# A prefill and decode layer with compensated one-pass products: last weight chunks of 21 input tiles and the narrow weights are split during the first feed-forward

## The chip, the cores and the metric

The kernel runs on one core of a Trainium2 chip. The metric is the device time of one launch in microseconds (us), as the median of several runs. PE is TensorE (matrix products), PEld its weight loads, DVE VectorE, ACT ScalarE, POOL GpSimd, SP SyncE, which here only issues transfers.

## The reference, cut to what matters

One layer of a hybrid decoder, in fp32, for 256 new tokens of one prompt and one new token each of 8 running sequences; together 264 columns:

```python
x = x + 0.5 * swiglu(rmsnorm(x, n1), f1g, f1u, f1d)      # 2048 -> 5504 -> 2048
h = rmsnorm(x, nm)
proj = h @ w_in                                          # 2048 -> 4864 columns
q, k, v = ...                                            # 16 query heads, 4 key/value heads of 64
o_att = attend(q, k, v, sinks)                           # window 128, sinks, relative bias
xm = proj + mu * (prev - proj)                           # token shift on the other 3328 columns
r, k, v, wl, al, gl = xm[...]
w = -softplus(-(w0 + tanh(wl) @ w2)) - 0.5               # decay:  64 -> 1024
a = sigmoid(a0 + al @ a2)                                # rate:   64 -> 1024
g = sigmoid(gl) @ g2                                     # gate:  128 -> 1024
S, y = wkv_scan(...)                                     # RWKV-7 state, 16 heads of 64
out = (groupnorm(y) + bonus) * g
x = x + concat(o_att, out) @ w_out
x = x + 0.5 * swiglu(rmsnorm(x, n2), f2g, f2u, f2d)
```

and a last rmsnorm; the new key/value windows, RWKV states and shift columns are outputs too.

## The kernel before, in words

All activations lie transposed: a tile holds 128 features by 264 columns, so the 2048 features are 16 tiles. Every large weight is used in 128 x 128 blocks. Each fp32 operand of a large product is written as a sum of two parts of the type fp32r, and three products of that type, which TensorE does as one instruction each, stand for the whole: hi x hi, hi x lo, lo x hi (`gemm`). Weights arrive in chunks of four blocks (128 x 512, 256 KB) over SyncE's queue into six buffers `raw`; ScalarE casts a chunk to `hi` (line 141) and VectorE subtracts to get `lo` (line 142 of the program, shown as its helper's line 68); there are four buffers of each (`chunk`). So a tile of a projection with 16 input tiles has 4 chunks and 48 products into one accumulator `acc`.

The program has three stages. The first feed-forward (`ffn`) goes over 43 hidden tiles in six parts: gate and up products for each hidden tile, then the down products of the part. Mixing (`mixing_body`) takes 38 tiles of `win`: tiles 0 and 1 are the inputs of decay, rate and gate, 2 to 25 the r, k, v of eight pairs of heads, 26 to 29 keys and values, 30 to 37 queries. The list `SEQ` sets their order: 0 to 19, then 26 to 33, then 20 to 25, then 34 to 37. After each chunk `tick` advances every running generator by one step, which strews the small work between the large products: `prep` for each pair (decay, rate, keys), `chain` for each batch of two pairs (the scan in blocks of 64), `attend` for each query tile, and so on. Then come the output projection and the second feed-forward. The engines' queues are filled in an order that a planner finds beforehand from estimated times; chunks have high priority in mixing.

Three products in mixing are done on plain fp32 operands, as one `mm` each, which TensorE's queue carries as two instructions: in `prep` the decay `tw` (65 rows: 64 of tanh(wl) and a row of ones that adds w0) and the rate `la` (128 rows, the first 64 meet zeros) by the pair's 128 x 256 weight `lw`; in `gnorm` the gate `sgl` by `g2s`. Their weights are loaded over SyncE's queue into a ring of `NLD` = 6 buffers `ld`, shared with the states, biases and cached keys. The block `o` holds squares for the norm at first and the eight query tiles later; block `e` is used late, by the output projection.

Of the kernel before, what the change touches and what calls it, by code (L numbers as in the profile page):

```python
# [7 lines left out]
F32 = mybir.dt.float32  # L8
F32R = mybir.dt.float32r
# [4 lines left out]
P = 128  # L14
# [15 lines left out]
NH, NQ, NT, NLD = 16, 8, 16, 6  # L30
# [21 lines left out]
VMU, VKK, VKA, VA0, VRK, VLW, VLB, VSK, VSD = 64, 90, 98, 106, 114, 122, 130, 138, 154  # L52
NVEC = 155
# [3 lines left out]
def body(tc, I, O):  # L57
# [51 lines left out]
    with ExitStack() as ctx:  # L109
# [35 lines left out]
        def gemm(ps, src, xs, step=None, rng=None, ahead=True, ready=None):  # L145
            n = len(xs)
            for k0 in range(0, n, CH):
# [3 lines left out]
                hi, lo = ready or chunk(src[:, k0 * P:k1 * P], k1 - k0, V, ahead)  # L151
# [160 lines left out]

        def first_ffn(n2):
# [8 lines left out]
            with tc.tile_pool(name="f1", bufs=1) as fp:  # L322
# [18 lines left out]
                ffn(n1, xr, I["gu1"], I["dn1"], nxt, load, more, None, first)  # L341
# [27 lines left out]
        def mixing_body(mx, n2, n3, XD, XR):  # L369
# [18 lines left out]
            tw = fix((65, T), "tw")  # L388
            G.memset(tw[64:65, :], 1.0)
# [8 lines left out]
            half = fix((P, 16), "half")  # L398
            ts(V, half, vec[:, VKA:VKA + 16], 0.5, ALU.mult)
# [30 lines left out]
            la, sgl = fix((P, T), "la"), fix((P, T), "sgl")  # L430
# [132 lines left out]
            def chain(bt):  # L563
# [121 lines left out]
                g2s = [load(I["g2"][bt.p0 + k], (P, P)) for k in range(n)]  # L685
# [16 lines left out]
            def gnorm(bt, pY, N, g2s):  # L702
# [207 lines left out]
            bat, att, bts, scores = [], [], [], []  # L910
            for kind, i in SEQ:
# [23 lines left out]
                else:  # L935
                    ps = win(LKV + 4 + i)
                    q = ob[i]
# [141 lines left out]

# [111 lines left out]
```

## Time and profile before

| | |
|---|---|
| median of 3 runs | 1935.28 us (1935.13 to 1935.48) |
| profiled execution | 1934.77 us, span 1932.9 us |
| granted TensorE clock | 0.998 |
| PE busy | 1919.4 us, 99% of the span |
| DVE, ACT busy | 1311.8 us (68%), 1023.7 us (53%) |
| DMA | 357 MB, 185 GB/s over the span |

The span runs from the first to the last instruction of the profiled execution; its own time has 1.9 us more around it. Busy time of an engine is the union of its instructions. A product's duration includes its way through the array, so successive products overlap and a mean duration is longer than the distance between their starts. In the chain of waits ("start us, length, what") each piece is followed back to what released it; a piece "PE acc L84 x61" is 61 products in a row that waited for nothing else. "<-" behind an idle time names what ended it.

### The profile page before, as it was taken

The page shows a single profiled execution, that of the slowest core. Times are in us where ns is not written, and L with a number is a line of the kernel's source. Part 1 is how long each engine was busy: PE and PEld are TensorE (multiplying, and loading weights), DVE is VectorE, ACT ScalarE, POOL GpSimd, SP SyncE. Part 2 cuts the span into 40 slices and gives each one's busy share as a digit, 9 for nine tenths or more (in the row PEclk, how much of TensorE's full clock was granted, in tenths as well). Part 3 has the DMA queues.
Part 4 walks back from the last instruction along what each step waited for, and adds up shares of the span by engine and source line. Part 5 has one row for each costly group of instructions (what it writes and reads, how often), then busy time and mean ns, then how long its engine had stood idle before and what let it go on. Part 6 is the DMA issues. An engine that isn't in the chain of part 4 may idle for free.

```text
span 1932.9 us, 45519 instructions
## 1 busy us (share of the span) xinstructions
PE 1919.4 (99%) x17171; PEld 1897.1 (98%) x17171; DVE 1311.8 (68%) x2606; ACT 1023.7 (53%) x2034; POOL 260.1 (13%) x376
## 2 busy tenths in 40 slices
PE   9999999999999999999999999999999999999998
PEld 9999999999999999999989999999999999999998
DVE  5865555655556568889988977866666666666665
ACT  5644444444444457675657555644444444444446
POOL 0401101011010113222102100300101001010012
PEclk9999999999999999999999999999999999999999
DMA  7666666666666668555646656666666666666664
GB/s 241 178 192 196 185 195 195 183 192 177 190 183 180 188 181 238 177 165 153 176 120 165 210 155 183 175 188 188 189 195 195 186 192 189 194 195 184 193 181 150
DMA packets 218464, 357.27 MB, mean 185 GB/s; under 512 B 33516, under 2 KB 71804, under 8 KB 218244
## 3 DMA queue, kind: packets, MB, share of 16 engines
q1 hardware_dynamic: 211936, 346.02, 60.8%
q10 hardware_dynamic: 6308, 8.35, 1.4%
q8 instruction: 134, 2.20, 0.4%
q14 instruction: 86, 0.70, 0.1%
HBM read 346.67 MB, written 9.69 MB: 184 GB/s over the span
## 4 chain that ended last, share of the span: by engine, by line
PE 96%; DVE 1%; ACT 1%; issue 1%; DMA 0%; POOLq 0%; POOL 0%; ACTq 0%; DVEq 0%
PE acc L84 89%; PE m L84 6%; DVE lo L68 0%; ACT t L78 0%; ACT hi L141 0%; DMA x<-in_x 0%; DVE t L801 0%; DVE st L68 0%; DVE Xt L68 0%; DMA ld<-in_bias 0%; ACT BT L533 0%; ACT L78 0%; POOLq L1187 0%; DVE PT L68 0%; PE m L528 0%
## 5 line engine op out<-in xcount | busy, mean ns | idle before, releaser
L68 DVE TENSOR_TENSOR lo<-raw,hi 128x512 fp32r<-128x512 f32 (+1 forms) x1288 | 874.0, 682 | 510.4 <-ACT hi L141 486.9
L141 ACT CAST hi<-raw 128x512 fp32r<-128x512 f32 (+1 forms) x1288 | 776.8, 606 | 820.2 <-PE acc L84 745.2
L84 PE MATMUL acc<-x,hi 128*128 128x264 f32 x4840 | 893.4, 286 | 0.8 <-ACT hi L141 0.8
L84 PEld LDWEIGHTS acc<-x,hi 128*128 128x128 f32 x4840 | 750.1, 189 | 4.3 <-ACT hi L141 1.0
L84 PE MATMUL acc<-x,lo 128*128 128x264 f32 x2420 | 691.3, 286 | 0.2 <-DVE lo L68 0.2
L84 PE MATMUL acc<-h,hi 128*128 128x264 f32 x2752 | 495.0, 284 | 0.0
L84 PEld LDWEIGHTS acc<-x,lo 128*128 128x128 f32 x2420 | 457.2, 189 | 2.7 <-issue 0.7
L84 PEld LDWEIGHTS acc<-h,hi 128*128 128x128 f32 x2752 | 424.4, 189 | 0.0
L84 PE MATMUL acc<-h,lo 128*128 128x264 f32 x1376 | 387.8, 284 | 0.0
L84 PEld LDWEIGHTS acc<-h,lo 128*128 128x128 f32 x1376 | 259.2, 189 | 0.0
L68 POOL TENSOR_TENSOR t<-t,t 128x264 f32<-128x264 f32 x74 | 79.8, 1078 | 1096.1 <-DVE t L68 949.8
L84 PE MATMUL acc<-y,hi 128*128 128x264 f32 x648 | 122.7, 284 | 0.0
L84 PE MATMUL acc<-o,hi 128*128 128x264 f32 x648 | 120.1, 284 | 0.0
L84 PE MATMUL acc<-kv,hi 128*128 128x264 f32 x582 | 109.8, 285 | 0.0
L84 PEld LDWEIGHTS acc<-y,hi 128*128 128x128 f32 x648 | 101.2, 189 | 0.1
L84 PEld LDWEIGHTS acc<-o,hi 128*128 128x128 f32 x648 | 100.1, 189 | 0.0
L71 DVE SCALAR_TENSOR_TENSOR x<-acc,x 128x264 f32<-128x264 f32 (+1 forms) x193 | 81.1, 425 | 24.3 <-PE acc L84 23.4
L84 PE MATMUL acc<-y,lo 128*128 128x264 f32 x324 | 92.0, 284 | 0.0
L84 PE MATMUL acc<-o,lo 128*128 128x264 f32 x324 | 92.0, 284 | 0.0
L84 PEld LDWEIGHTS acc<-kv,hi 128*128 128x128 f32 x582 | 89.9, 189 | 0.2
L68 DVE TENSOR_TENSOR t<-acc,t 128x264 f32<-128x264 f32 x156 | 67.4, 432 | 32.9 <-PE acc L84 32.9
L84 PE MATMUL acc<-kv,lo 128*128 128x264 f32 x291 | 82.9, 285 | 0.0
(307 smaller groups left out, 1592.5 us busy)
## 6 DMA issues: line engine op xcount, KB each, us to landing
raw<-in_gu SPq DMA_DIRECT2D x688, 256.0 KB, 3.4
raw<-in_dn SPq DMA_DIRECT2D x224, 256.0 KB, 2.9
raw<-in_win SPq DMA_DIRECT2D x152, 256.0 KB, 3.4
raw<-in_dn SPq DMA_DIRECT2D x160, 192.0 KB, 2.8
raw<-in_wout SPq DMA_DIRECT2D x64, 256.0 KB, 3.5
xsp<-x ACTq DMA_DIRECT2D x16, 132.0 KB, 3.4
x<-xsp SPq DMA_DIRECT2D x16, 132.0 KB, 4.2
ld<-in_sT SPq DMA_DIRECT2D x16, 128.0 KB, 3.6
```

The lines of the kernel that those rows point to most:

```text
L68: return e.tensor_tensor(out=out, in0=a, in1=b, op=op)
L71: return V.scalar_tensor_tensor(out=out, in0=a, scalar=s, in1=b, op0=op0, op1=op1)
L84: return TE.matmul(out, lhsT, rhs, start=start, stop=stop, **k)
L141: A.copy(hi[:, :w], raw[:, :w])
```

## The change

Four things change together.

1. `split_early` is a generator that the first feed-forward advances once per hidden tile from its second part on. Each step loads one 128 x 512 piece of weights (`er`), splits the piece loaded a step before (`eh`, `el`), and stores the parts that were split a step before that to DRAM. The first six pieces are the weights of decay, rate and gate (`low`); the other 21 are the last of the four chunks of tiles 3 to 19 and 26 to 29 of `win` (`AHEAD`, stored in `kept`). That is 27 loads, 27 splits and 54 stores.
2. In mixing, `win` fetches for each of these tiles both parts of its last chunk (128 x 1024, 512 KB, one transfer) one tile ahead into one of two halves of block `o`, and `gemm` uses them in place of a `chunk`. The query tiles take block `o` only when the first of them is computed.
3. The narrow products become one-pass. `lor` holds, for each of decay and rate, the high part of its 64 rows above their low part; the weight is stored twice, one below the other, so one product over 128 rows takes in both parts, and two (weight high, weight low) make the whole. The gate takes three products. w0 moves from a row of ones to the bias of the activation.
4. `NLD` becomes 8.

The queues, taken from the planned programs. First TensorE where the first pair's `prep` makes its decay and rate products (the names in a row are output <- moving operand, weight; `acc` is the win tile under way, the numbers are buffer names). Before:

```order
L84 MATMUL acc_10837<-x_106,lo_10840 128x264
L84 MATMUL m_10858<-tw,ld_10856 128x264
L84 MATMUL m_10860<-la,ld_10856 128x264
L84 MATMUL acc_10837<-x_107,hi_10872 128x264 x2
L84 MATMUL acc_10837<-x_107,lo_10873 128x264
```

and in the change:

```order
L85 MATMUL acc_11053<-x_108,lo_11057 128x264
L85 MATMUL m_11077<-e_10644,ld_11073 128x264
L85 MATMUL m_11077<-e_10644,ld_11075 128x264
L85 MATMUL m_11078<-e_10644,ld_11073 128x264
L85 MATMUL m_11078<-e_10644,ld_11075 128x264
L85 MATMUL acc_11053<-x_109,hi_11093 128x264 x2
L85 MATMUL acc_11053<-x_109,lo_11094 128x264
```

Two rows of plain fp32 (two instructions each) become four one-pass rows, `m_11077` the decay and `m_11078` the rate, at the same place in the tile. The gate of the first pair, in the change, with buffer numbers:

```order
L85 MATMUL acc2570_13685<-x32_108,hi2572_13687 128x264
L85 MATMUL m2520_13395<-gate0_10645,ld2466_13139 128x264
L85 MATMUL m2520_13395<-gate1_10646,ld2466_13139 128x264
L85 MATMUL m2520_13395<-gate0_10645,ld2467_13141 128x264
L85 MATMUL acc2570_13685<-x32_108,hi2572_13687 128x264
```

One row of plain fp32 has become three: high by high, low by high, high by low. Where the first kept chunk is used, TensorE's queue now reads it from block `o`:

```order
L85 MATMUL acc_10905<-x_110,hi_10944 128x264 x2
L85 MATMUL acc_10905<-x_110,lo_10945 128x264
L85 MATMUL acc_10905<-x_110,hi_10944 128x264 x2
L85 MATMUL acc_10905<-x_110,lo_10945 128x264
L85 MATMUL acc_10905<-x_111,o_10825 128x264 x12
L85 MATMUL acc_10979<-x_108,hi_10982 128x264 x2
```

The twelve products of that chunk follow those of the third chunk as before; only their source is another.

Second, SyncE's queue at the start of mixing (loads of `raw` are chunks, `ld` the ring). Before:

```order
L378 DMA ld_10856<-in_lw 128x256
L140 DMA raw_10637<-in_win 128x512
L378 DMA ld_11150<-in_lw 128x256
L140 DMA raw_10655<-in_win 128x512
L378 DMA ld_11414<-in_sT 128x256
L378 DMA ld_11416<-in_sT 128x256
L140 DMA raw_10680<-in_win 128x512
L378 DMA ld_11422<-in_sT 128x256
L378 DMA ld_11424<-in_sT 128x256
L140 DMA raw_10698<-in_win 128x512
```

In the change:

```order
L403 DMA ld_11073<-low 128x256
L141 DMA raw_10863<-in_win 128x512
L403 DMA ld_11075<-low 128x256
L141 DMA raw_10881<-in_win 128x512
L403 DMA ld_11356<-low 128x256
L403 DMA ld_11358<-low 128x256
L141 DMA raw_10907<-in_win 128x512
L443 DMA o_10825<-kept 128x1024 x2
L141 DMA raw_10925<-in_win 128x512
L403 DMA ld_11614<-in_sT 128x256
L403 DMA ld_11616<-in_sT 128x256
L403 DMA ld_11622<-in_sT 128x256
```

The narrow weights of the first two pairs are now two loads each, and the first two fetches of kept chunks stand between the chunks of the fourth tile, which has three chunks here. Later each fetch has a place of its own:

```order
L141 DMA raw_11165<-in_win 128x512
L141 DMA raw_11203<-in_win 128x512
L141 DMA raw_11221<-in_win 128x512
L141 DMA raw_11263<-in_win 128x512
L443 DMA o_10825<-kept 128x1024
L141 DMA raw_11281<-in_win 128x512
L141 DMA raw_11299<-in_win 128x512
L141 DMA raw_11338<-in_win 128x512
```

This fetch, the third, is for tile 5 and waits for the last product of tile 3, whose half it overwrites; ahead of it stand the chunk loads up to the first of tile 7. Counted through the whole queue, from the third fetch to the last there are 9 or 10 chunk loads ahead that belong to later tiles than the one waited for.

Third, SyncE's queue in the first feed-forward, around one step of `split_early`:

```order
L141 DMA raw_4215<-in_gu 128x512
L141 DMA raw_4233<-in_gu 128x512
L322 DMA kept<-eh_4101 128x512
L322 DMA kept<-el_4102 128x512
L141 DMA raw_4271<-in_gu 128x512
L332 DMA er_4269<-in_win 128x512
L141 DMA raw_4289<-in_gu 128x512
L141 DMA raw_4307<-in_gu 128x512
```

The two stores of one step stand together between the chunk loads of two hidden tiles, and the load of the next step follows one chunk load later; before the change there are only the chunk loads.

The diff, without the renumbering of a few columns and lines:

```diff
-NH, NQ, NT, NLD = 16, 8, 16, 6
+NH, NQ, NT, NLD = 16, 8, 16, 8
...
+AHEAD = [*range(3, 20), *range(26, 30)]
...
-        def gemm(ps, src, xs, step=None, rng=None, ahead=True, ready=None):
+        def gemm(ps, src, xs, step=None, rng=None, ahead=True, ready=None, kept=None):
...
-                hi, lo = ready or chunk(src[:, k0 * P:k1 * P], k1 - k0, V, ahead)
+                hi, lo = kept if kept and k1 == n else ready or chunk(src[:, k0 * P:k1 * P], k1 - k0, V, ahead)
...
+        def split_early(fp):
+            todo = [(I["win"][t][:, 12 * P:], [kept[i, :, e] for e in range(2)]) for i, t in enumerate(AHEAD)]
+            todo = [(I["low"][:, q * 512:(q + 1) * 512], [low[:, 2 * q:2 * q + 2, e] for e in range(2)]) for q in range(6)] + todo
+            raw, parts, keep = [], [], tc.keep_in_program_order
+            while todo or raw or parts:
+                if parts:
+                    to, both = parts.pop()
+                    for d, x in zip(to, both):
+                        keep(SP.dma_start(d, x.bitcast(F32) if len(d.shape) == 2 else x.bitcast(F32).rearrange("p (k c) -> p k c", k=2)))
+                if raw:
+                    to, x = raw.pop()
+                    hi, lo = (fp.tile([P, CH * P], F32R, tag=n, bufs=2, name=uid(n)) for n in ("eh", "el"))
+                    A.copy(hi, x)
+                    tt(V, lo, x, hi.bitcast(F32), ALU.subtract)
+                    parts.append((to, (hi, lo)))
+                if todo:
+                    src, to = todo.pop(0)
+                    x = fp.tile([P, CH * P], F32, tag="er", bufs=2, name=uid("er"))
+                    keep(SP.dma_start(x, src))
+                    raw.append((to, x))
+                yield
...
-                ffn(n1, xr, I["gu1"], I["dn1"], nxt, load, more, None, first)
+                side = split_early(fp)
+                ffn(n1, xr, I["gu1"], I["dn1"], nxt, load, more, side, first)
...
+            early = {}
+
+            def fetch(i):
+                if i >= len(AHEAD):
+                    return
+                if not early:
+                    early[None] = sp.tile([P, 8 * ROW], F32, tag="o", bufs=1, name=uid("o"))
+                x = early[None][:, 16 + i % 2 * 8 * P:16 + (i % 2 + 1) * 8 * P]
+                with tc.high_priority():
+                    SP.dma_start(x.rearrange("p (e c) -> p e c", e=2), kept[i])
+                early[AHEAD[i]] = [x[:, e * CH * P:(e + 1) * CH * P].bitcast(F32R) for e in range(2)]
+
             def win(t):
                 ps = acc()
-                gemm(ps, I["win"][t], n2.xs, tick)
+                if t + 1 == AHEAD[0] or t in AHEAD:
+                    fetch(AHEAD.index(t) + 1 if t in AHEAD else 0)
+                gemm(ps, I["win"][t], n2.xs, tick, kept=early.get(t))
...
-            la, sgl = fix((P, T), "la"), fix((P, T), "sgl")
+            lor = blk("e", 2, F32R)
+            gate = [mx.tile([P, T], F32R, name=f"gate{i}") for i in range(2)]
+
+            def parts(src):
+                return [load(src[:, e], (P, 256)).bitcast(F32R) for e in range(2)]
...
-                lw = load(I["lw"][p], (P, 256))
-                zp = mp()
-                mm(zp[:, :T], lw[0:65, 0:P], tw[0:65, :])
-                ap = mp()
-                mm(ap[:, :T], lw[:, P:2 * P], la)
+                lw = parts(low[:, p])
+                zp, ap = mp(), mp()
+                for j, ps in enumerate((zp, ap)):
+                    for i, w in enumerate(lw):
+                        mm(ps[:, :T], w[:, j * P:(j + 1) * P], lor[j], i == 0, i == 1)
                 sg, a = tmp(), tmp()
-                act(sg, zp[:, :T], AF.Tanh, scale=0.5)
+                act(sg, zp[:, :T], AF.Tanh, scale=0.5, bias=half[:, 16 + p:17 + p])
...
-                g2s = [load(I["g2"][bt.p0 + k], (P, P)) for k in range(n)]
+                g2s = parts(low[:, NPAIR + bt.i])
...
-                    mm(gp[:, :T], g2s[k], sgl)
+                    c = slice(k * P, (k + 1) * P)
+                    mm(gp[:, :T], g2s[0][:, c], gate[0], True, False)
+                    mm(gp[:, :T], g2s[0][:, c], gate[1], False, False)
+                    mm(gp[:, :T], g2s[1][:, c], gate[0], False, True)
...
-            shifted(0, la)
-            act(tw[0:64, :], la[0:64, :], AF.Tanh)
-            shifted(1, sgl)
+            la = shifted(0, tmp())
+            act(la[0:64, :], la[0:64, :], AF.Tanh)
+            for r, x in zip(HALF, lor):
+                A.copy(x[0:64], la[r])
+                tt(V, x[64:128], la[r], x[0:64].bitcast(F32), ALU.subtract)
+            sgl = shifted(1, tmp())
             act(sgl, sgl, AF.Tanh, scale=0.5)
             ts(G, sgl, sgl, 0.5, ALU.mult, 0.5, ALU.add)
+            A.copy(gate[0], sgl)
+            tt(V, gate[1], sgl, gate[0].bitcast(F32), ALU.subtract)
...
+                    ob = ob or blk("o", 8)
...
+        low = dp.tile([P, NPAIR + len(BATCH), 2, 256], F32, tag="low", name="low")
+        kept = dp.tile([len(AHEAD), P, 2, CH * P], F32, tag="kept", name="kept")
```

More of the change, by code (lines that the diff above doesn't have):

```diff
@@ L51 @@
 VG1, VGM, VG2, VGF = 0, 16, 32, 48
-VMU, VKK, VKA, VA0, VRK, VLW, VLB, VSK, VSD = 64, 90, 98, 106, 114, 122, 130, 138, 154
-NVEC = 155
+VMU, VKK, VKA, VA0, VW0, VRK, VLW, VLB, VSK, VSD = 64, 90, 98, 106, 114, 122, 130, 138, 146, 162
+NVEC = 163
 CID, CBO, CCM, CMK = 0, 128, 256, 384
@@ L339, in more @@
                     xr.extend(xg[:, j] for j in range(4))
-                ffn(n1, xr, I["gu1"], I["dn1"], nxt, load, more, None, first)
+                side = split_early(fp)
+                ffn(n1, xr, I["gu1"], I["dn1"], nxt, load, more, side, first)
+                assert next(side, side) is side
         def dec_state(fp, XR):
@@ L397, in mixing_body @@
                 G.tensor_copy(unit[i * 32:i * 32 + 32, :], ident[i * 32:i * 32 + 32, i * 32:i * 32 + 32])
-            half = fix((P, 16), "half")
-            ts(V, half, vec[:, VKA:VKA + 16], 0.5, ALU.mult)
+            half = vec[:, VKA:VKA + 24]
+            ts(V, half, half, 0.5, ALU.mult)
             less = fix((P, 8), "less")
@@ L1144, in layout @@
     a["shs"] = c(i["state_shift"][0][:, sc].reshape(NB, NSH, P).transpose(2, 1, 0))
-    lw = np.zeros((8, P, 256), f4)
-    lw[:, :64, :P] = i["decay_w2"][0].reshape(64, 8, P).transpose(1, 0, 2)
-    lw[:, 64, :P] = i["decay_w0"][0].reshape(8, P)
-    lw[:, 64:, P:] = i["aaa_a2"][0].reshape(64, 8, P).transpose(1, 0, 2)
-    a["lw"] = lw
-    a["g2"] = c(i["gate_g2"][0].reshape(P, 8, P).transpose(1, 0, 2))
+    w2, a2 = (i[n][0].reshape(64, 8, P) for n in ("decay_w2", "aaa_a2"))
+    low = np.stack([np.concatenate([x, x], 0) for x in (w2, a2)], 2).reshape(P, 2 * 8 * P)
+    a["low"] = c(np.concatenate([low, i["gate_g2"][0]], 1))
     bk = _buckets()
```

5 lines of the change are left out of this document (2 added, 3 removed).

## The prediction

> **What bounds the kernel now.** First the page's busy shares and its chain of waits, then the same by stage, then what TensorE waits for inside the stage that the change touches. The stages are: first feed-forward to 751 us, mixing 751 to 1150, second feed-forward after that. In mixing the program takes its 38 input tiles in the order 0 to 19, 26 to 33, 20 to 25, 34 to 37; the 21 tiles of the change are the fourth to the twenty-fourth taken, and by their products they run from 769 to 923 us.
>
> The page, parts 1 and 4:
>
> ```profile
> PE 1919.4 (99%) x17171; PEld 1897.1 (98%) x17171; DVE 1311.8 (68%) x2606; ACT 1023.7 (53%) x2034; POOL 260.1 (13%) x376
> ...
> PE 96%; DVE 1%; ACT 1%; issue 1%; DMA 0%; POOLq 0%; POOL 0%; ACTq 0%; DVEq 0%
> ```
>
> The same by stage: window, its length, then the busy time of PE, PEld, DVE, ACT and POOL with their instructions, the granted clock, the DMA share and GB/s:
>
> ```profile
> 66.00:751.00 685.00, 685.00 (x5711) 685.00 (x5710) 415.71 (x706) 341.45 (x614) 87.97 (x88) 1.00 0.64 190
> 751.00:923.00 172.00, 171.66 (x1782) 166.64 (x1781) 145.44 (x344) 111.83 (x269) 46.01 (x113) 1.00 0.60 175
> 923.00:1061.00 138.00, 135.31 (x1717) 124.80 (x1716) 119.20 (x365) 91.76 (x250) 19.23 (x53) 1.00 0.54 150
> 1061.00:1150.00 89.00, 89.00 (x1010) 84.07 (x1010) 75.00 (x228) 48.21 (x121) 7.47 (x14) 1.00 0.63 182
> ```
>
> The reader is to see that TensorE is the bound, not only on average but in the stretch that is relieved: between 751 and 923 it is idle for 172.00 - 171.66 = 0.34 us, although VectorE is busy for 85% of it. The next stretch, 923 to 1061, has 2.69 us of idle TensorE; the change moves no split out of it. In the first feed-forward, which takes up the moved work, TensorE is never idle.
>
> What TensorE and its weight loads wait for between 751 and 1150 (total us, times, longest):
>
> ```profile
> PE m L808 <- DVE PT L68: 1.2, 1, 1.2
> PE m L755 <- issue: 0.7, 1, 0.7
> ...
> PEld m L84 <- issue: 3.0, 12, 0.4
> PEld m L808 <- issue: 1.4, 1, 1.4
> PEld m L84 <- ACT kr L544: 1.3, 3, 0.6
> ```
>
> Waits for a split (lines 141 and 68) are absent or a few tenths; the only wait for a busy ScalarE of any size is for the copy at L544, 1.3 us.
>
> **The change part by part.** *The narrow products.* Before, each of the eight pairs makes two products of four-byte operands (tw and la) and one for the gate (sgl). Each takes two instructions:
>
> ```profile
> L84 PE MATMUL m<-tw,ld 65*128 65x264 f32 x16 | 5.3, 412 | 0.0
> L84 PE MATMUL m<-la,ld 128*128 128x264 f32 x16 | 5.1, 399 | 0.3 <-ACT kr L544 0.2
> L84 PE MATMUL m<-sgl,ld 128*128 128x264 f32 x16 | 4.5, 386 | 0.0
> ```
>
> Their mean durations (0.39 to 0.41 us) overlap each other, so they are not the price. The price is the time that such a group occupies in the chain (start, length, what):
>
> ```profile
> 65.79 691.23 PE acc L84 x5760
> ...
> 801.40 0.90 PE m L84 x4
> ...
> 929.85 0.45 PE m L84 x2
> ```
>
> The piece at 801.40 is one pair's tw and la products, 0.90 us; the one at 929.85 is one gate product, 0.45 us. So a four-byte product of 264 columns costs 0.45 us, and the 24 of them 10.8 us. The first row prices the form that replaces them: 691.23 / 5760 = 0.120 us for each one-pass product of the same width with its own weight load. The change issues 8 x 4 for decay and rate and 8 x 3 for the gate, 56 x 0.120 = 6.7 us. All of it lies on TensorE's own path, with nothing beside it: **-4.1 us**. (That a new product takes more than one pass is unlikely: it is the form of the first row. Of the gain 8 x 0.42 = 3.4 comes from the pairs and 8 x 0.09 = 0.7 from the gates.)
>
> *21 chunk splits leave mixing.* What goes is 21 casts on ScalarE and 21 subtractions on VectorE at these means:
>
> ```profile
> L68 DVE TENSOR_TENSOR lo<-raw,hi 128x512 fp32r<-128x512 f32 x1128 | 786.7, 700 | 492.8 <-ACT hi L141 469.4 <-PE acc L84 7.5
> L141 ACT CAST hi<-raw 128x512 fp32r<-128x512 f32 x1128 | 697.2, 619 | 745.0 <-PE acc L84 684.9 <-PE m L84 22.3 <-DVE t L68 11.3
> ```
>
> 13.0 us of ScalarE and 14.7 us of VectorE, out of 111.8 and 145.4 busy. But they lay beside TensorE's products, and the relief can return only what TensorE waits there. Upper bound: 0.34 us of idle engine, or, counting by the waits for weight loads, the 1.3 us behind L544. Two of those three waits stand right before a pair's la product, and splits stand in ScalarE's queue ahead of the copy:
>
> ```profile
> 823.99 0.37 ACT hi L141
> ...
> 825.79 0.51 ACT t L78
> 826.30 0.51 ACT hi L141
> 826.81 0.06 ACT XD L546
> 826.87 0.28 ACT kr L544
> 827.15 0.04 issue
> 827.20 0.71 PE m L84 x2
> ```
>
> With one split in four gone, one such wait of about half a microsecond may vanish. Lower bound 0; I take **-0.5 us**, between the two, because the rows show a split on each of these short chains but not which one goes. The weight products of the kept chunks stay 12 per tile at the same width, hence no change there.
>
> *27 splits, 27 loads and 54 stores enter the first feed-forward.* 27 x 0.62 = 16.7 us on ScalarE (341 of 685 busy), 27 x 0.70 = 18.9 us on VectorE (416 of 685). One split enters per hidden tile, which has 96 products or 11.5 us. In 11.5 us there is a slack of about 4.5 us on VectorE and 5.8 on ScalarE, so 0.7 and 0.62 fit. The bytes are 81 x 0.26 MB = 21 MB, or about 31 GB/s more over the stage, to some 220. That more than this can be moved with TensorE unhindered is shown by
>
> ```profile
> 1070.00:1080.00 10.00, 10.00 (x106) 9.03 (x104) 9.54 (x40) 7.09 (x23) 0.01 (x1) 1.00 0.89 278
> ```
>
> The stores sit in SyncE's queue a whole hidden tile behind their split, so nothing there waits for them. Cost 0; if the cover were gone, a split costs TensorE at most its 0.7 us, 27 times, 19 us.
>
> *Mixing reads 21 x 512 KB instead of 21 x 256 KB.* Each fetch sits in SyncE's queue and waits for the last product of the tile two before its own, since there are two halves. Behind it stand the ordinary chunk loads. By the order of the changed program, 9 or 10 chunks of loads past that product stand ahead of each fetch (from the third on). A chunk is 12 x 0.12 = 1.44 us, so TensorE has 13 us of work ahead. A held-up load needs its landing and its split:
>
> ```profile
> raw<-in_win SPq DMA_DIRECT2D x152, 256.0 KB, 3.4
> ...
> X<-sa SPq DMA_DIRECT2D x4, 512.0 KB, 4.8
> ```
>
> 3.4 + 0.62 + 0.70 = 4.7 us, less than 13; the fetch itself lands in about 4.8 us (the row of the same size) and has some 10 us. Cost 0. The tightest place is the start of mixing, where the first two fetches and two more narrow weights join a dense stretch:
>
> ```profile
> 757.00:767.00 10.00, 10.00 (x84) 9.93 (x83) 7.57 (x14) 8.04 (x16) 4.44 (x18) 1.00 0.82 245
> ```
>
> One megabyte more in ten microseconds is 345 GB/s; at a share of 0.82 for 245 the engines would be full at about 299 (an estimate from this row), so loads land some 1.5 us later. The first fetch waits for the sum of squares behind the first tile, and nine chunks past that tile are ahead of it in the queue: 13 us against 4.7 + 1.5, so 0 again, at worst 1.5 us. Three more casts and three more subtractions of 264 columns there take 1.2 us of engines that have 2 us free in that row.
>
> **Sum.** -4.1 - 0.5 = -4.6 us. The profiled execution took 1934.77 us (span 1932.9 and 1.9 around it), so 1930.2; the median of the runs is 1935.28, 0.5 above it, so **1930.7**. A measurement of this kernel can tell 0.2%, 3.9 us, from no change; the line is at 1931.4, close to the forecast.
>
> **The rivals.** *A larger gain from relieved engines.* The weight loads are idle for 172.00 - 166.64 = 5.4 us in the relieved stretch, far more than the 0.34 of the products. If splits caused all of it, the time is 1935.3 - 4.1 - 5.4 = 1925.8. Against it: the same small group costs the same wherever it stands,
>
> ```profile
> 816.15 2.46 PE m L84 x34
> ...
> 862.02 2.46 PE m L84 x34
> ...
> 926.14 2.46 PE m L84 x34
> ```
>
> which is a price and not a wait, and such groups hold idle weight loads. The Trainium skill (Perfetto Trace Analysis, "Identifying the Most-Contended Engine") says that matmul busy time is no good measure of how near TensorE is to its limit and that the busy share of weight loads is better; by that rule the headroom is the 5.4 us. The repeated 2.46 speaks against reading all of it as headroom. Chance 0.10.
>
> *The shorter products come to nothing where others set the pace.* Between 923 and 1061 VectorE is busy for 119 of 138 us and TensorE already waits. Two pairs and six gates are made there or near it, 2 x 0.42 + 6 x 0.09 = 1.4 us; if TensorE only arrives earlier at the same wait, this is lost, and with no relief elsewhere the gain is 2.7: 1932.6. For it: the wait for L808 is VectorE's. Against it: all idle there is 2.69 us, in few places. Chance 0.18.
>
> *Slower: fetches hold up SyncE's queue.* The rows of that queue show that it does wait for products before small loads:
>
> ```profile
> SPq L378 <- PE m L84: 7.8, 10, 1.8
> ```
>
> Were each of 21 fetches to hold the queue so long that the next chunk is half a microsecond late for TensorE, 21 x 0.5 = 10.5 us come on: 1935.3 - 4.1 + 10.5 = 1941.7. It decides once the loads ahead are worth less than the 4.7 us of a landing and a split, under four chunks; the order shows nine. The Trainium skill (DMA: Bandwidth & Descriptors, "Queues, rings and completion order") says that descriptors of one queue are taken in ring order on each DMA engine, so a 512 KB fetch delays the loads behind it by its own transfer. That rule speaks against the change; from the 278 GB/s above it would be 1.9 us per fetch instead of 0.9, still inside the 13 us. Chance 0.10, with stalls from the stores in the first feed-forward counted in.
>
> **How the numbers follow.** The forecast's own case has 0.62, of which 0.56 under 1931.4 and 0.06 above; with the larger gain 0.10: faster 0.66. No change: 0.06 + 0.18 = 0.24. Slower 0.10. Low end: all 3.0 us of idle TensorE from 751 to 1061 go, 1935.3 - 4.1 - 3.0 = 1928.2, put at 1928.0; high end: the second rival with half a microsecond lost at the start of mixing, 1933.2. Outside lie the first and third rivals, 0.2.
>
> **What would show it.** The group of four narrow products should take 0.48 us where two took 0.90, three gate products 0.36. The split's casts in mixing should be 21 fewer, and TensorE's idle time in the first 172 us of mixing should stay near 0.3. The first feed-forward must still end at 751 us with TensorE idle for nothing; a later end, or a fetch of a kept chunk as the releaser of a product, makes the forecast wrong upwards. If mixing shrinks by over 7 us, weight-load idle was headroom and the first rival holds.

## The result, and the profile after

The changed kernel takes 1965.5 us (median of 5 runs, 1962.23 to 1967.83) against 1935.48 (1935.13 to 1936.87) for the kernel before on the same chip: 1.015 times, with a 95% interval of 1.0139 to 1.0161. It is slower by some 30 us, and the forecast was 1930.7. The profiled execution took 1962.23 us with a span of 1960.4, so 27.5 us more span than before. By the starts of the window products, the first feed-forward ends at 781.3 instead of 751.1 (+30.2), mixing takes 422.9 instead of 426.0 (-3.1), and the rest 756.3 instead of 755.9 (+0.4). The sum of these is the 27.5.

Busy shares and chain of waits on the page after:

```profile
PE 1927.2 (98%) x17179; PEld 1899.6 (97%) x17179; DVE 1307.8 (67%) x2615; ACT 1018.9 (52%) x2043; POOL 247.6 (13%) x375
...
PE 88%; DMA 6%; DVE 2%; ACT 2%; issue 1%; SPq 1%; DVEq 0%; ACTq 0%
```

TensorE's share of the chain fell from 96% to 88%, and DMA, which had none, has 6%. VectorE and ScalarE are no busier than before. The first feed-forward and the relieved stretch of mixing (window, length, busy time of PE, PEld, DVE, ACT and POOL, clock, DMA share, GB/s):

```profile
66.00:781.20 715.20, 696.36 (x5713) 689.30 (x5712) 421.15 (x734) 346.84 (x641) 86.70 (x88) 1.00 0.68 212
781.20:950.50 169.30, 169.02 (x1779) 164.85 (x1779) 135.92 (x321) 101.85 (x252) 36.86 (x114) 1.00 0.70 220
```

In the first feed-forward TensorE now idles for 715.20 - 696.36 = 18.8 us, and is busy for 11 us longer, in products that follow each other late. Some 1.7 of these are the clock: for 3.41 us from 556.7 on, just behind a wait of 1.8 us, the granted clock was half (hence the 0.98 of part 5 below). Such stretches come back in mixing. ScalarE is busy for 347 of 715 us there, so it isn't short of time. The gate and up products of parts 2 to 6, after:

```profile
146.50:232.50 86.00, 82.90 (x674) 81.28 (x673) 47.24 (x81) 40.35 (x75) 12.48 (x12) 1.00 0.72 232
272.80:363.60 90.80, 83.77 (x674) 81.46 (x673) 45.71 (x77) 40.34 (x75) 12.03 (x12) 1.00 0.72 225
404.00:493.90 89.90, 83.56 (x675) 81.50 (x674) 45.76 (x77) 40.37 (x75) 12.39 (x12) 1.00 0.70 223
534.20:620.00 85.80, 83.43 (x675) 82.37 (x674) 46.20 (x76) 40.61 (x74) 12.54 (x12) 0.98 0.72 227
660.30:740.90 80.60, 80.60 (x674) 80.60 (x673) 44.90 (x71) 39.49 (x69) 12.74 (x12) 1.00 0.54 183
```

Before, every one of the five took 80.6 or 80.7 us. Part 6, in which the side work has run out, still does; parts 2 to 5 lose 5.4, 10.2, 9.2 and 5.2 us. The down products between them take 40.3 us as before. What ScalarE waited for from 146 to 640 us (total us, times, longest), first rows:

```profile
ACT hi L142 <- PE acc L85: 136.5, 191, 1.7
ACT eh L326 <- DMA er<-in_win: 84.9, 21, 6.3
ACT eh L326 <- DMA er<-in_low: 19.6, 5, 4.9
```

The first row is the ordinary one: ScalarE is ahead and waits for a free buffer. The other two are new: it stands 104.5 us over 26 casts, 4.0 us each, until the side piece `er` has landed. TensorE's own waits, from 146 to 781 us, are for the casts and subtractions of chunks, which come late:

```profile
PE acc L85 <- ACT hi L142: 13.9, 13, 2.2
PE acc L85 <- DVE lo L69: 4.7, 16, 0.3
```

Before the change there is no such wait. The transfers by the page (KB each, median us from issue to landing):

```profile
raw<-in_gu SPq DMA_DIRECT2D x688, 256.0 KB, 3.5
...
o<-kept SPq DMA_DIRECT2D x21, 512.0 KB, 4.7
er<-in_win SPq DMA_DIRECT2D x21, 256.0 KB, 6.0
```

The chunk loads land as they did (3.4 before), the piece of the same size takes 6.0. One step in order of time, SyncE's issues first, then ScalarE (start us, us, what, idle before and its releaser):

```profile
285.25 0.42 SPq L322 DMA_DIRECT2D kept<-eh  x1
285.72 0.42 SPq L322 DMA_DIRECT2D kept<-el  x1
286.24 0.43 SPq L141 DMA_DIRECT2D raw<-in_gu  x1
286.72 1.00 SPq L332 DMA_DIRECT2D er<-in_win  x1
...
287.82 0.62 ACT L142 CAST hi<-raw 128x512 fp32r<-128x512 f32 x1 [0.47 <-PE acc L85]
293.83 0.62 ACT L326 CAST eh<-er 128x512 fp32r<-128x512 f32 x1 [5.38 <-DMA er<-in_win]
294.35 1.14 ACT L142 CAST hi<-raw 128x512 fp32r<-128x512 f32 x2
```

`er` is issued at 286.72 and lands at 293.75. ScalarE has it next in its queue at 288.45, 1.7 us after the issue, and stands 5.38 us. Behind it wait the casts of chunks, and behind those the buffers `raw` that they would free. The planned programs show why the cast comes so early. The rows 225 to 229 of SyncE's queue and 288 to 293 of ScalarE's, both in the changed kernel:

```
L322 DMA kept<-eh_3937 128x512
L322 DMA kept<-el_3938 128x512
L141 DMA raw_4107<-in_gu 128x512
L332 DMA er_4105<-in_win 128x512
L141 DMA raw_4125<-in_gu 128x512

L142 CAST hi_4034<-raw_4033 128x512
L326 CAST eh_4265<-er_4105 128x512
L142 CAST hi_4052<-raw_4051 128x512
L142 CAST hi_4070<-raw_4069 128x512
L79 ACTIVATE t_4089<-t_4087 128x264
L142 CAST hi_4108<-raw_4107 128x512
```

On SyncE `er_4105` follows the chunk `raw_4107`; on ScalarE its cast stands three chunk casts ahead of that chunk's. The loads of chunks run some six ahead of their casts, and this piece is denied half of that lead. The program writes the split one hidden tile after the load, but what was built has it three chunks early, in nearly every step.

### The profile page after: what moved, and what is told of

It is laid out like the page before. It is cut to its first block, busy times and chain, and to the rows that moved or that the text cites. A ratio compares the mean times of both kernels' runs of the same rounds, so it can differ in the third digit from the quotient of the medians.

```text
span 1960.4 us, 45655 instructions
## 1 busy us (share of the span) xinstructions
PE 1927.2 (98%) x17179; PEld 1899.6 (97%) x17179; DVE 1307.8 (67%) x2615; ACT 1018.9 (52%) x2043; POOL 247.6 (13%) x375
## 4 chain that ended last, share of the span: by engine, by line
PE 88%; DMA 6%; DVE 2%; ACT 2%; issue 1%; SPq 1%; DVEq 0%; ACTq 0%
PE acc L85 81%; PE m L85 7%; DMA raw<-in_gu 4%; DMA er<-in_win 2%; DVE lo L69 1%; ACT hi L142 0%; ACT t L79 0%; SPq L141 0%; DMA xsp<-x 0%; DMA x<-in_x 0%; SPq L322 0%; ACT eh L326 0%; PE m L569 0%; DMA raw<-in_win 0%; PE m L852 0%
## 5 line engine op out<-in xcount | busy, mean ns | idle before, releaser
L69 DVE TENSOR_TENSOR lo<-raw,hi 128x512 fp32r<-128x512 f32 (+1 forms) x1267 | 856.0, 682 | 436.2 <-ACT hi L142 416.2
L142 ACT CAST hi<-raw 128x512 fp32r<-128x512 f32 (+1 forms) x1267 | 756.9, 605 | 723.9 <-PE acc L85 645.6
L85 PE MATMUL acc<-x,hi 128*128 128x264 f32 x4672 | 868.7, 286 | 14.3 <-ACT hi L142 14.1
L85 PEld LDWEIGHTS acc<-x,hi 128*128 128x128 f32 x4672 | 725.5, 189 | 22.1 <-ACT hi L142 17.9
L85 PE MATMUL acc<-x,lo 128*128 128x264 f32 x2336 | 668.1, 286 | 5.1 <-DVE lo L69 5.0
L85 PEld LDWEIGHTS acc<-x,lo 128*128 128x128 f32 x2336 | 442.0, 189 | 10.2 <-DVE lo L69 9.2
L69 DVE TENSOR_TENSOR el<-er,eh 128x512 fp32r<-128x512 f32 x27 | 18.7, 693 | 103.7 <-ACT eh L326 103.7
```

Source lines behind the costliest of these rows:

```text
L69: return e.tensor_tensor(out=out, in0=a, in1=b, op=op)
L85: return TE.matmul(out, lhsT, rhs, start=start, stop=stop, **k)
L142: A.copy(hi[:, :w], raw[:, :w])
```

## The experiments

**The theories.** A: the cast stands in ScalarE's queue before what it needs has landed, and everything behind it is late. B: the stores' bytes on the same queue slow the chunk loads. C: the added casts and subtractions are themselves too much.

**The cast a step later in the text, and the load ahead of the stores.** The first edit, with three buffers `er`, and the second, which moves the load's block ahead of the stores:

```diff
-                if raw:
-                    to, x = raw.pop()
+                if len(raw) > 1 or raw and not todo:
+                    to, x = raw.pop(0)
```

```diff
             while todo or raw or parts:
+                # load of the next piece, as below, issued here
                 if parts:
                     # two stores
                 if raw:
                     # cast, subtraction
-                if todo:
-                    # load
```

> The changed kernel, with the side split a step later: ScalarE's cast of a side piece is written two hidden tiles behind its load instead of one (three buffers er instead of two). Same loads, same stores, same queue, same 27 splits. In ScalarE's queue the cast of er then stands behind 3 to 5 chunk casts that are loaded after er, where in the changed kernel it stands ahead of 3 chunk casts that were loaded before it; only the first two of the 27 steps keep their old place. Theory A (the side cast stands in ScalarE's queue before its load has landed, and the chunk casts behind it are late): the loss of the first feed-forward, 30.2 us over 27 steps or 1.1 us a step, goes but for those two steps; it ends at 751 to 755 and the time is 1932 to 1937. Theory B (the two 256 KB stores of a step slow the chunk loads that follow on the same queue, wherever the cast stands) and theory C (the added casts and subtractions themselves are too much): nothing changes, the first feed-forward ends at 775 to 782, time 1957 to 1963.

> The changed kernel, with the load of a side piece issued ahead of the step's two stores instead of behind them. The cast keeps its place in ScalarE's queue (3 chunk casts nearer than er's load on SyncE's queue), and the bytes are the same. Theory A: what counts is when er lands; with 512 KB less ahead of it it should land in about 4 to 4.5 us (raw<-in_gu beside it 3.5) instead of 6.0, ScalarE's stand of some 2.4 us falls to under 1, and of the 30.2 us at most 10 remain: first feed-forward ends at 752 to 762, time 1933 to 1944. Theory B: the stores still stand ahead of the chunk loads, so nothing changes: 775 to 782, time 1957 to 1963. Theory C: nothing changes either.

Measured: late cast 1943.51 us (1.0041 times before, 1.0026 to 1.0056), first feed-forward to 762.4; load first 1962.86 us (1.0132, 1.0112 to 1.0153), to 779.2. The first undid 18.9 of the 30.2 us, which C and B exclude, but 11.3 stayed, where A had forecast 4 at most; the second undid 2, where A had forecast 20 or more. What the two waited for, 146 to 640 us; late cast:

```profile
ACT eh L326 <- DMA kept<-eh: 65.1, 19, 4.8
ACT eh L326 <- DMA low<-eh: 16.6, 6, 3.4
...
DVE el L69 <- DMA kept<-el: 15.3, 4, 5.1
```

and load first:

```profile
ACT eh L332 <- DMA kept<-eh: 64.2, 19, 5.2
ACT eh L332 <- DMA low<-eh: 14.5, 5, 3.6
...
DVE el L69 <- DMA low<-el: 18.0, 4, 5.4
DVE el L69 <- DMA kept<-el: 15.2, 4, 4.9
```

The casts no longer wait for `er`, but for the store that empties the buffer `eh` into which they write; there are two such buffers, and the store of two steps before is not through. Theory A has to say: the cast must stand behind the landing of both. It was wrong in naming `er` alone.

That the load gained little from its place (5.5 us in the median against 6.0) is explained by what the DMA engines do around the step. Slices of one microsecond in the changed kernel:

```profile
288.00:289.00 1.00, 1.00 (x11) 1.00 (x10) 0.52 (x1) 0.45 (x1) 0.35 (x1) 1.00 1.06 367
289.00:290.00 1.00, 1.00 (x10) 1.00 (x10) 0.17 (x1) 0.00 (x0) 0.00 (x0) 1.00 1.03 387
290.00:291.00 1.00, 1.00 (x11) 1.00 (x10) 0.00 (x0) 0.00 (x0) 0.00 (x0) 1.00 1.02 342
```

The share of the stage is 0.68, but for three microseconds behind this group of stores the engines are full at 342 to 387 GB/s. The Trainium skill (DMA: Bandwidth & Descriptors, "Where 436 GB/s comes from") gives about 358 GB/s as the limit between HBM and SBUF. The three slices average 365 GB/s, and two of them lie above that figure.

**Without the stores of the window pieces.** `split_early` leaves them out, and mixing splits its own chunks.

```diff
-                if t + 1 == AHEAD[0] or t in AHEAD:
+                if False:
```

> The changed kernel without the stores of the 21 window pieces: they are loaded and split in the first feed-forward as before, but not stored, and mixing loads and splits its chunks itself. The six low-rank pieces are stored and used. The cast stands 4 chunk casts nearer than its load in most of the 21 steps (3 in the changed kernel). Theory A: er lands faster without stores ahead of it (about 3.5 to 4 us), but meets a cast some 1.4 us earlier, so some stand is left, up to 1 us a step: part 2 keeps its 5.4 us, parts 3 to 5 lose 0 to 15 of 24.6: first feed-forward ends at 757 to 771. Theory B: parts 3 to 5 lose nothing: 757. Theory C: they lose what they lost: 775 to 782. Mixing loses what the kept pieces brought it, 0 to 3 us.

Measured: 1944.43 us (1.0049, 1.0034 to 1.0064). Part 2 still loses 5.2 us, parts 3 to 5 nothing; the first feed-forward ends at 756.5. `er` now lands in 4.3 us. Mixing took 430.2 us, 7.3 more than in the changed kernel, where 0 to 3 had been forecast; some 5.1 of them were stretches at half clock (see below). ScalarE's stand:

```profile
ACT eh L328 <- DMA er<-in_win: 53.2, 21, 5.0
ACT eh L328 <- DMA er<-in_low: 18.4, 5, 4.8
```

2.5 us for a window piece cost nothing, 3.7 us for a low-rank piece (whose stores are still there) cost 0.9 us a step, the changed kernel's 4.0 cost 1.1. So the buffers absorbed 2.5 us; what they do between 2.5 and 3.7 was not measured. It speaks against C, but cannot part A from B, since both blame the stores.

**The cast placed.** The cast is ordered behind a product that was written five chunks earlier (`done` collects the last product of each chunk). This sets the order in the queue and adds no semaphore.

```diff
-    def behind(i):
-        tc.add_manual_dep(i.ins, big[0].ins.name, ...
+    def behind(i, at=None):
+        tc.add_manual_dep(i.ins, (at or big[0]).ins.name, ...
...
+                done.append(big[0])
...
-                    A.copy(hi, x)
+                    behind(A.copy(hi, x), done[-5])
```

> The changed kernel with the place of the side cast in ScalarE's queue set by hand: it is put behind a product five chunks before the end of the hidden tile ahead, by an order without a semaphore. In ScalarE's queue the cast then stands 5 to 6 chunk casts behind the chunk load that er's load follows on SyncE's queue, where in the changed kernel it stands 3 chunk casts ahead of that; 8 places later, that is 8 x 1.44 = 11.5 us. Loads, stores, their order, the two buffers er, eh and el and all bytes are those of the changed kernel. Late cast alone left 11.3 us of the 30.2: there ScalarE stood 65.1 us over 19 casts for the stores that empty eh, as theory A in its new form has it: the cast must stand where both have landed, its own er and the store that emptied its eh two steps before. Here both have some 15 us. Theory A: ScalarE stands for eh less than 5 us in all, the first feed-forward ends at 751 to 754, mixing keeps its 422.8, time 1931.5 to 1935. Theory B (the stores slow the chunk loads behind them): 10 us or more of the loss stay, the first feed-forward ends at 762 or later, time 1942 or more.

Measured: **1932.24 us (1930.95 to 1933.82), 0.9983 times before, 0.9974 to 0.9992**. It beats both kernels. The first feed-forward as one window:

```profile
66.00:751.20 685.20, 685.20 (x5712) 685.20 (x5711) 432.17 (x734) 355.77 (x641) 87.65 (x88) 1.00 0.72 221
```

The landing of `er` from 146 to 640 us:

```profile
DMA to landing us min/median/max: 4.2/5.8/6.9
```

One step in order of time, SyncE's issue and ScalarE's casts:

```profile
279.34 0.96 SPq L334 DMA_DIRECT2D er<-in_win  x1
...
293.37 0.62 ACT L143 CAST hi<-raw 128x512 fp32r<-128x512 f32 x1 [0.47 <-PE acc L86]
293.89 0.61 ACT L328 CAST eh<-er 128x512 fp32r<-128x512 f32 x1
```

The stage ends at 751.2 and TensorE idles for nothing, as before. Loads, stores and bytes are those of the changed kernel, `er` lands no sooner, and the stage's traffic is 221 GB/s instead of 212, in less time. Only the cast is later: 14.5 us after the issue instead of 1.7, and nothing waits for it. That is A, and the end of B and C. The Trainium skill (PSUM — Partial Sum Buffer, "Engine vs sequencer instructions") says that ScalarE's queue is strictly first in, first out; the traces agree, since chunk casts stood 5.4 us behind one that was not ready. The Trainium skill's advice (DMA: Bandwidth & Descriptors, "Rules for kernel authors") to issue a transfer early and wait for it late is what this edit does.

**Four buffers `eh` and `el`,** the cast in the changed kernel's place (`bufs=2` becomes `bufs=4`).

> The changed kernel with four buffers eh and el instead of two, the cast in its place of the changed kernel (3 chunk casts ahead). The cast then waits for no store, only for its own er, which lands in 6.0 us. It tells which of the two landings holds ScalarE. Theory A, if er is the later one: ScalarE still stands 3.5 to 4.2 us a step, first feed-forward ends at 771 to 782, time 1951 to 1963. Theory A, if the store is: the stand falls to the 2.4 us that it was without stores, which cost nothing there: 751 to 760 behind the part-2 loss of 5.4, so 757 to 765, time 1937 to 1946. Theory B: nothing changes, 775 to 782.

Measured: 1964.3 us (1.0154, 1.0138 to 1.0169), first feed-forward to 781.6.

```profile
ACT eh L326 <- DMA er<-in_win: 76.5, 21, 6.1
ACT eh L326 <- DMA er<-in_low: 19.0, 5, 5.4
```

With no store to wait for, ScalarE still stands 3.7 us a cast (4.0 in the changed kernel), and the stage still loses 30 us, up to 6.8 of them in stretches at half clock (1.7 in the changed kernel): there it is the load that lands last. The late cast and the load first made it the store.

**Mixing: each half of the change alone.** The narrow products alone have `AHEAD = []` and no fetch; once with the cast as in the changed kernel, once placed. The kept pieces alone are the kernel before with the 21 pieces and the cast placed.

> The one-pass low-rank and gate products alone: six side pieces (the low-rank and gate weights) are loaded, split and stored in part 2 of the first feed-forward, and no window piece is. By the forecast's own step the narrow products take 4.1 us from mixing; all theories have the six steps cost what part 2 lost, 5.4 us. So the first feed-forward ends at 755 to 757 and, if the 4.1 us come true, mixing takes 422 and the time is 1936.5; if the shorter products come to nothing, mixing takes 426 and the time is 1940.7. If all of the 3.1 us that mixing won in the changed kernel is theirs, mixing takes 422.9 and the kept window pieces are worth nothing.

> The narrow products alone (six side pieces, no kept window piece) with the cast placed. By theory A the 5.0 us that these six steps cost the first feed-forward go: it ends at 751. If mixing's 428.8 is a matter of the order within it, and that order is not touched by the cast, mixing takes 428.8 again and the time is 1935.3 + 2.8 = 1938; by the forecast's term alone it would be 1931.2.

> The kernel before with the 21 kept window pieces alone, the side cast placed as in the run before; low-rank and gate products stay four-byte products. By the forecast's step the 21 splits that leave mixing bring 0.5 us: mixing 425.5, time about 1935. By the runs so far (mixing 428.8 with the narrow products alone, 422.9 with both) the kept pieces bring 5.9 us: if that holds without the narrow products, mixing takes 420 and the time is 1929.5. If they only take away waits that the narrow products bring in, mixing takes 425 to 426. First feed-forward as in the run before: 751 to 754 by theory A, 760 or later by theory B.

Measured: narrow alone 1943.56 us (1.0044, 1.0029 to 1.0059), first feed-forward to 756.1; narrow placed 1939.18 us (1.0018, 1.0008 to 1.0027), to 751.3; kept alone 1937.89 us (1.0013, 1.0005 to 1.0022), to 751.3. Neither half gains; together and placed they do. Mixing took 428.8 us with the narrow products alone, where 422 to 426 had been forecast, and 429.0 with the kept pieces alone, where 420 to 426 had been. Mixing as a whole, by the sums over its windows (length, then busy time), for the kernel before, narrow alone, kept alone, and both placed:

```profile
sum 426.00, PE 422.97 PEld 402.52 DVE 361.37 ACT 265.74 POOL 72.61; mean PE 211.49 PEld 201.26 DVE 180.69 ACT 132.87 POOL 36.31
```

```profile
sum 428.80, PE 420.61 PEld 401.03 DVE 362.24 ACT 267.30 POOL 65.86; mean PE 210.30 PEld 200.52 DVE 181.12 ACT 133.65 POOL 32.93
```

```profile
sum 429.00, PE 424.64 PEld 403.65 DVE 351.83 ACT 254.95 POOL 59.68; mean PE 212.32 PEld 201.83 DVE 175.92 ACT 127.47 POOL 29.84
```

```profile
sum 423.10, PE 419.02 PEld 400.01 DVE 351.54 ACT 255.43 POOL 61.60; mean PE 209.51 PEld 200.01 DVE 175.77 ACT 127.72 POOL 30.80
```

Narrow alone, TensorE is busy for 2.4 us less and idles for 8.2 us instead of 3.0. Its longest waits there:

```profile
PE m L852 <- DVE PT L69: 2.8, 1, 2.8
PE m L85 <- ACT BT L574: 2.2, 2, 1.6
PE m L85 <- ACT W L651: 1.8, 1, 1.8
```

These are links of the state chain between VectorE, ScalarE and TensorE. They sit in three tiles: the 27th, 28th and last of the 38 taken are 12.1, 14.7 and 15.5 us apart, where both placed have 8.9, 10.2 and 12.7.

TensorE also runs slower for a while behind such a wait. The wait of 2.8 us, and two windows of 3.4 us behind it:

```profile
970.50:973.30 2.80, 0.01 (x2) 0.03 (x1) 2.57 (x11) 2.20 (x9) 0.61 (x3) 1.00 0.54 177
974.00:977.40 3.40, 3.40 (x18) 3.40 (x17) 3.26 (x15) 0.84 (x2) 0.00 (x0) 0.50 0.32 77
977.40:980.80 3.40, 3.40 (x42) 2.87 (x42) 2.92 (x11) 0.99 (x2) 0.00 (x0) 1.00 0.31 82
```

At a granted clock of 0.50 there are 18 products, at 1.00 in the same time 42 (not all of one shape). The traces of all twelve kernels have 15 such stretches ahead of the kernel's end, each 3.41 or 6.83 us long, so that up to 1.7 or 3.4 us are lost in it. Each starts during a wait of TensorE or within some 2 us behind one, of 0.7 us or more. Not every wait has one: those of 1.8 us in mixing of the changed kernel and of the cast placed have none. That the wait brings the half clock on fits all 15, and was not tried.

**How many kept pieces?** The cast placed, with `AHEAD` of 17 (`range(3, 20)`) and of 8 (`range(3, 11)`).

> The changed kernel with the cast placed (as in the run of that name), but only the 17 window pieces of tiles 3 to 19 are kept; tiles 26 to 29 split their own. Mixing took 428.8 with the narrow products and no kept piece, 423.1 with 21, and 429.0 with 21 kept pieces and the four-byte products: neither part gains alone. Theory P (each kept piece takes a cast and a subtraction from ScalarE and VectorE, on which the side work waits): 428.8 - 17 x 0.27 = 424.2. Theory Q (the place of the side work's small products among the window products, fixed when the program is built, comes out otherwise in each build, and with it some waits of 1 to 3 us): no trend; TensorE busy 419 to 421 as in the two with narrow products, and the rest is idle time in a few places, mixing anywhere from 422 to 430. The first feed-forward ends at 751 by both.

> As the run with 17, with the 8 pieces of tiles 3 to 10 alone. Theory P: mixing takes 428.8 - 8 x 0.27 = 426.6. Theory Q: no trend, 422 to 430, TensorE busy 419 to 421. The first feed-forward ends at 751 by both.

Measured: with 17 pieces 1937.42 us (1.001, 1.0 to 1.0021), with 8 1937.93 us (1.0012, 1.0001 to 1.0022); both first feed-forwards end at 751.2. Mixing in the profiled executions, 17 pieces:

```profile
751.20:1176.80 425.60, 420.45 (x4737) 400.96 (x4736) 353.68 (x960) 257.55 (x649) 65.69 (x178) 1.00 0.62 183
```

8 pieces, and none (narrow placed, whose profiled execution took 1941.2 us, 2.0 above its median):

```profile
751.20:1178.60 427.40, 420.75 (x4737) 401.33 (x4736) 357.54 (x969) 263.01 (x658) 66.04 (x178) 1.00 0.61 177
```

```profile
751.30:1183.20 431.90, 425.25 (x4738) 405.12 (x4737) 362.74 (x977) 267.53 (x666) 65.74 (x178) 0.98 0.58 171
```

Part of these differences is the clock, though 1.7 us in some 425 still reads as 1.00 in a row of the whole stage. Mixing in the profiled executions, in us; the last column is the length less the idle time and the loss at half clock:

| kernel | length | TensorE idle | lost at half clock | TensorE's work |
|---|---|---|---|---|
| before | 426.0 | 3.0 | 0 | 423.0 |
| kept pieces alone, placed | 429.0 | 4.4 | 1.7 | 422.9 |
| narrow alone | 428.8 | 8.2 | 1.7 | 418.9 |
| narrow alone, placed | 431.9 | 6.7 | 6.8 | 418.4 |
| both, 8 pieces | 427.4 | 6.7 | 1.7 | 419.0 |
| both, 17 pieces | 425.6 | 5.2 | 1.7 | 418.7 |
| both, 21 pieces (cast placed) | 423.1 | 4.1 | 0 | 419.0 |
| the changed kernel | 422.9 | 4.2 | 0 | 418.7 |

TensorE's work is 423 us with four-byte narrow products and 418.4 to 419.0 with one-pass ones, whatever is kept. The builds differ in their waits and in the half clock behind some of these. The clock is not a matter of the profiled executions alone: the ten runs of narrow placed have a mean granted clock of 0.9959, the kernel before beside them 0.9984. That is 0.0025 x 1936 = 4.8 us (an estimate, as each run's clock is given to 0.001), more than the 3.5 us by which the medians differ.

The waits are 6.7 us without kept pieces (8.2 in the other such build), 6.7 with 8, 5.2 with 17 and 4.1 with 21. P's sizes, 426.6 and 424.2, were 0.8 and 1.4 too short; Q's range of 422 to 430 holds both lengths too. By the medians none, 8 and 17 pieces can't be told apart (1.0018, 1.0012 and 1.001), and only the 21 stand out. So neither theory is shown. The same 21 pieces beside four-byte products made mixing 3.0 us longer, 1.3 in waits and 1.7 at half clock. Why the waits come out so is open: the place of the small products among the window products differs between these builds, and no run changed that alone.

## Why the prediction was wrong, step by step

**The step that failed** is the cost 0 of the 27 splits, loads and stores in the first feed-forward; it was 30.2 us. The prediction counted cover as free time of an engine ("In 11.5 us there is a slack of about 4.5 us on VectorE and 5.8 on ScalarE, so 0.7 and 0.62 fit"). The time was free: with the cast placed the same work costs 0.1 us. But an engine that works in order has no free time ahead of an instruction that isn't ready, and the prediction never set the cast's place in ScalarE's queue against the load's place in SyncE's. It looked at what the stores wait for in SyncE's queue, and not at what is queued behind the cast in ScalarE's. Its bound of 19 us was too low for the same reason: it priced the duration of a split, 0.7 us, and not the landing of its load, 6.0 us.

**The traffic** was right: 31 GB/s more, forecast to some 220, measured 221 against 190 with the cast placed. That the mean share leaves room did not say that a group of two stores and several loads has any: in the slices above it fills the engines for three microseconds.

**The narrow products.** The group of four takes 0.48 us and six gate products 0.73, as forecast. In the chain of the changed kernel:

```profile
812.99 0.48 PE m L85 x4
...
1170.56 0.73 PE m L85 x6
```

So TensorE's own saving is 8 x (0.90 - 0.48) + 8 x (0.45 - 0.36) = 4.1 us, and TensorE's work in the table fell by 4.0 to 4.6. Mixing did not always shrink by it: alone, the waits grew by 5.2 us and 1.7 were lost at half clock, so mixing became 2.8 us longer. The waits are the second rival's mechanism (others set the pace), and more of it than the rival had; the clock nobody had reckoned with.

**The 21 splits that leave mixing** were put at a gain of 0.5 us, at most 1.3. With the narrow products in, mixing is 5.7 us shorter for them (428.8 to 423.1), 4.1 in waits and 1.7 at half clock; without them it is 3.0 longer. The bound was taken from TensorE's waits in the kernel before, in the stretch from which the splits go. The gain lies later, in the three tiles named above, in waits that the other half of the change brings in. Against the kernel before, both halves together left TensorE 1.1 us more of idle time, where 0.5 less was forecast. The splits did go, 77 casts instead of 97 in the stretch where they stood:

```profile
L141 ACT CAST hi<-raw 128x512 fp32r<-128x512 f32 x97 | 59.0, 617 | 32.7 <-PE acc L84 27.5 <-ACT t L426 2.5 <-DVE st L68 0.8
L142 ACT CAST hi<-raw 128x512 fp32r<-128x512 f32 x77 | 46.9, 617 | 34.0 <-PE acc L85 21.5 <-issue 6.8 <-ACT t L463 2.1
```

Of the two terms' sum, -4.6, mixing has -2.9 to -3.1: the first term came true as work, and the second had the wrong sign. That the cast placed, at 1932.24, comes near the forecast of 1930.7 is in part luck: in its profiled execution mixing has no stretch at half clock, and in those of the other placed kernels, with a half or with fewer pieces, it has one or more.

**The fetches of 512 KB** cost nothing, as forecast: they land in 4.7 us (the row of the same size had 4.8) and none appears among the releasers of a product. The third rival had them hold SyncE's queue and put the stores' stalls into the same 10.5 us. The side was right, the mechanism was not: with the same fetches and stores in the same order the cast placed loses nothing, and the loss was three times as large.

**The weight loads' idle time** was no headroom: in the relieved stretch it was 5.4 us of 172 and is 4.45 of 169.3, so the first rival falls.

## What to carry to other kernels

Work that is added beside a full pipeline is sure to cost nothing only if each of its instructions is ready when its engine reaches it (here a stand of 2.5 us a step was absorbed, one of 3.7 was not). For every added instruction, count the instructions between its place in its engine's queue and the place at which its input was issued, price them, and set that against the landing of the input and of whatever empties its output buffer. The row to look for is a wait of a side instruction on an engine that is half idle. Where the order is fixed when the program is built, read the built order, since the written one can differ, and place the instruction by hand if it must be late.

## What the runs showed that was not expected

Mean DMA use says little about a landing. At a mean share of 0.68 a 256 KB load beside two 256 KB stores took 6.0 us and one ahead of them 5.5, against 3.5 for the loads around; without the stores 4.3.

A stand of ScalarE of 2.5 us in each hidden tile cost TensorE nothing, 3.7 us cost 0.9 and 4.0 cost 1.1. The length of the stand does not settle it alone: late cast and load first had ScalarE stand equally long (85 us in all) and lost 11.3 and 28.1 us. VectorE stood 15.3 us for the store of `el` in the first and 33.2 in the second; that this makes the difference was not tried.

Two halves of a change that each made the kernel slower by 0.1 to 0.2% with the cast placed made it 0.17% faster together. In mixing of the profiled executions the halves lost 1.7 and 6.8 us in stretches at half clock, each behind a wait of TensorE, and the two together none. On the engine that bounds the kernel a short wait went with a loss of more than its own length.
